# Four of the eight gated-convolution column tiles computed as block pairs in the pair stage, and a chunk loop whose exponentials are issued ahead of its fill

## The chip, the cores and the metric

The kernel runs on one core of one Trainium2 chip. The metric is the device time of one execution in microseconds, as the median of several runs. On the core, TensorE (PE) multiplies matrices, VectorE (DVE) and ScalarE (ACT) work elementwise, GpSimd (POOL) does the rest of the elementwise work, and SyncE (SP) issues the DMAs.

## The reference, cut to what matters

One layer of a hybrid decoder: a token mixer with two branches that read the same normalised input `h` (1024 positions, 1024 channels), then a gated MLP.

```python
proj = h @ w_in
z, xbc, dt_raw, sc_b, sc_c, sc_h, gates = jnp.split(proj, points, axis=-1)
y_ssd = ssd_branch(z, xbc, dt_raw, ...) @ w_ssd_out
y_sc = short_conv_branch(sc_b, sc_c, sc_h, sc_conv_w) @ w_sc_out
g_ssd, g_sc = jnp.split(jax.nn.sigmoid(gates), 2, axis=-1)
mix = (g_ssd * y_ssd + g_sc * y_sc) @ w_o

def short_conv_branch(b_gate, c_gate, h, conv_w):
    return b_gate * causal_dwconv(c_gate * h, conv_w)      # three taps
```

`ssd_branch` is a chunked scan: 4 groups of 8 heads, 8 chunks of 128 positions each. Inside a chunk the scores are weighed with exponentials of differences of a running sum, and a state is carried from chunk to chunk. The change is about the three column groups `sc_b`, `sc_c` and `sc_h` (each 1024 wide, so 8 tiles of 128 columns), and about the chunk loop.

## The kernel before, in words

Every float32 product is made of three matmuls on operands split into a high and a low part (`split`, lines 129 to 131: ACT casts the high part, DVE subtracts).

**The pair stage** (lines 583 to 628) computes two column tiles of `w_in` together. `Pair` (line 178) splits the product into 2 by 2 blocks and needs seven block products where eight would be the direct way. A block product (`product`, line 166) is 12 matmuls of 128x128 by 512, so a pair is 84 matmuls, where two tiles computed directly (`gemm`, line 158, 48 matmuls each) are 96. For this the pair needs sums of weight blocks (line 193, DVE) and seven weight splits of 512 columns (lines 130 and 131), and it takes its results from PSUM with ACT copies (line 218) and DVE additions (lines 235, 252, 256). The stage runs its pairs in the order of a string of letters (line 621): z (gate of the scan), g (merge gates) and x (scan inputs, with a four-tap convolution of 3 DVE instructions per tile).

**The chunk loop** (lines 805 to 818) runs over 32 chunks. Chunk n+1's front (`ssd_front`, line 677) loads its decay tile `E` (line 690, one of two buffers), transposes and scales the inputs. Then some steps of the fill run, then chunk n's back (`ssd_back`, line 730: 32 or 16 matmuls of line 737 into `y`, the state of lines 747 to 755, the norm of the chunk before, the output of lines 765 to 767, its square and two additions, lines 769 to 771), and then chunk n+1's decay (`ssd_decay`, line 710: exponentials on ACT at lines 716 to 726, two multiplications on DVE at lines 717 and 727, one on POOL at line 723).

**The fill** is the gated convolution: `sc_tile` (line 776) computes three column tiles directly with 48 matmuls each, and gives control back after each half (24 matmuls). `STEPS` (line 805) says how many halves run in each of eight chunks: 10 in 8 chunks, 40 in the loop. The last 8 halves run after the loop (line 822). Each column tile costs a weight split on ACT and DVE, and the three of one index share two multiplications, a copy and three taps (lines 780 to 794).

After the loop the branches (line 876) read `y_d` and `ysc_d` back from DRAM, split them (lines 842 to 853), and multiply with the output weights.

The program is written as a sequence, and a planner orders each engine's instructions by what is ready; so the order of a trace differs from that of the text. All DMAs go through SP's queue in order.

Of the kernel before, what the change touches and what calls it, by code (L numbers as in the profile page):

```python
# [8 lines left out]
F32 = mybir.dt.float32  # L9
# [3 lines left out]
ALU = mybir.AluOpType  # L13

P = 128
# [7 lines left out]
EPS = 1e-6  # L23

# [9 lines left out]
def hybrid_kernel(ctx: ExitStack, tc: tile.TileContext, x, pack, row_p, ada_w, w_in,  # L34
# [582 lines left out]

    zs = [(z_pair, g, j) for g in range(NG) for j in (0, 2)]
    xs = [(xbc_pair, g, j) for g in range(NG) for j in (0, 2, 4)]
    gs = [(gate_pair, 0, 2 * n) for n in range(8)]  # L620
    for kind in "zzggggggggxxzxzxxzxxzxxzxxzx":
        fn, g, j = dict(z=zs, x=xs, g=gs)[kind].pop(0)
        fn(g, j)
        if steps is not None:
            if next(steps, steps) is steps:
                steps = None
            last[1] = steps is not None
# [25 lines left out]
    pend = []  # L653

    late = []
# [54 lines left out]
    def ssd_decay(front):  # L710
# [3 lines left out]
        if c > 0:  # L714
            Cs = sw.tile([P, 8, P], F32, tag="Cs", name=f"Cs{nm}", bufs=2)
            S.activation(Cs, E, AF.Exp)  # L716
            V.tensor_tensor(Cs, Cs, xb[:, 5, cs].unsqueeze(1).to_broadcast([P, 8, P]), op=ALU.mult)
# [3 lines left out]
        if c < NCH - 1:  # L721
            xw = sw.tile([P, 8, 64], F32, tag="xw", name=f"xw{nm}")
# [3 lines left out]
        S.activation(E, E, AF.Exp, scale=-1.0)  # L726
        V.tensor_tensor(E, E, sm.unsqueeze(1).to_broadcast([P, 8, P]), op=ALU.mult)  # L727
        return Cs, cd, xw

    def ssd_back(front, decay):  # L730
# [37 lines left out]
        sq = scratch.rearrange("p (a b) -> p a b", a=4)  # L768
        S.activation(sq, y2, AF.Square, scale=512 ** -0.5)
        V.tensor_tensor(sq[:, 0:2, :], sq[:, 0:2, :], sq[:, 2:4, :], op=ALU.add)  # L770
        V.tensor_tensor(sq[:, 0, :], sq[:, 0, :], sq[:, 1, :], op=ALU.add)
        pend.append((sq, y2, nm, yo, g, c))
# [3 lines left out]
    def sc_tile(i):  # L776
        W = load_split(w_in[41 + i * 3], f"wsc{i}")
        pc = yield from gemm(A1p, W, f"scc{i}")
        ct = evt(f"sct{i}")
        S.copy(ct, pc)  # L780
        yield
        W = load_split(w_in[41 + i * 3 + 1], f"wsh{i}")
        ph = yield from gemm(A1p, W, f"sch{i}")
        V.tensor_tensor(ct, ph, ct, op=ALU.mult)
        w = cv["sc_w"][:, i * 3:i * 3 + 3]
        u = evt(f"scu{i}")
        S.activation(u, ct, AF.Copy, scale=w[:, 2:3])
        for k in (1, 0):
            s = 2 - k
            V.scalar_tensor_tensor(u[:, s:], ct[:, :T - s], w[:, k:k + 1], u[:, s:], op0=ALU.mult, op1=ALU.add)  # L790
        yield
        W = load_split(w_in[41 + i * 3 + 2], f"wsb{i}")
        pb = yield from gemm(A1p, W, f"scb{i}")
# [523 lines left out]
```

## Time and profile before

| | us |
|---|---|
| median of 3 runs | 2043.41 (2042.09 to 2044.56) |
| the profiled execution | 2045.67 |
| its span, first to last instruction | 2044.0 |
| PE / DVE / ACT / POOL busy | 1993.1 / 1453.3 / 978.8 / 152.0 |

The busy times are read against the span. A stage's share says more than that of the whole, so the rows further down cut the span into the stretches that the change touches. In this trace a matmul's duration includes the time in which the next one already runs, so the price of a matmul is read from one start to the next.

### The profile page before, as it was taken

The numbers are of one execution on the slowest core, as the hardware profiler recorded it, in microseconds if no ns is written. First come the engines' busy times: TensorE is split into PE (matmuls) and PEld (weight loads), VectorE is DVE, ScalarE is ACT, GpSimd is POOL, SyncE is SP. The second block draws the span as 40 slices with busy tenths as digits, with TensorE's granted clock in tenths as the row PEclk, the third lists the DMA queues.
The fourth block names the chain that finished last, engine by engine and source line by source line (L and its number), as shares of the span: only waits on it lengthen the run. The fifth ranks groups of instructions, "written<-read, shape, count | busy, mean of one in ns | idle before, by whom it ended". The sixth has DMA issues, their size and how long they took to land. (4 is left out here: it accounts for less than half of the span.)

```text
span 2044.0 us, 25283 instructions
## 1 busy us (share of the span) xinstructions
PE 1993.1 (98%) x9476; PEld 1599.2 (78%) x9476; DVE 1453.3 (71%) x2016; ACT 978.8 (48%) x1572; POOL 152.0 (7%) x183
## 2 busy tenths in 40 slices
PE   7999999999999999999999999999999999989997
PEld 3788888888887777777887878876888888868886
DVE  4966567767768787786766555378887777767876
ACT  4665455544547656554422442246554454544443
POOL 1200000000002222121000010021000000000002
PEclk9999999999999999999999999999999999999999
DMA  8233223233245556553686567252222222268362
GB/s 298 77 125 120 104 98 120 100 111 120 99 139 208 167 186 206 170 165 127 203 275 230 196 228 266 93 187 71 103 72 93 83 73 93 83 228 282 119 232 98
DMA packets 128426, 308.97 MB, mean 151 GB/s; under 512 B 11184, under 2 KB 40240, under 8 KB 128304
## 3 DMA queue, kind: packets, MB, share of 16 engines
q1 hardware_dynamic: 128304, 307.36, 43.9%
q8 instruction: 74, 1.21, 0.2%
q14 instruction: 48, 0.39, 0.1%
HBM read 241.65 MB, written 65.67 MB: 150 GB/s over the span
## 5 line engine op out<-in xcount | busy, mean ns | idle before, releaser
L1042 DVE SCALAR_TENSOR_TENSOR uv<-u_u,pk,uv 128x1023 f32<-128x1023 f32 (+1 forms) x88 | 107.2, 1279 | 7.4 <-ACT uv L1039 7.4
L130 ACT CAST u_t_hi<-u_t 128x512 fp32r<-128x512 f32 x88 | 54.7, 623 | 119.8 <-PE u_p L172 108.6
L130 ACT CAST wy_hi<-wy_raw 128x1024 fp32r<-128x1024 f32 x32 | 33.6, 1051 | 133.4 <-PE bps L858 83.4
L594 DVE SCALAR_TENSOR_TENSOR xv<-x_u,pk,xv 128x1023 f32<-128x1023 f32 (+2 forms) x72 | 87.1, 1279 | 4.9 <-ACT xv L591 4.9
L725 ACT ACTIVATE E<-E,tokS 128x128 f32<-128x128 f32 x256 | 80.5, 390 | 14.5 <-DMA E<-acs_d 13.8
L130 ACT CAST u_hi<-u_raw 128x512 fp32r<-128x512 f32 x66 | 41.0, 622 | 73.2 <-PE u_p L172 73.2
L131 DVE TENSOR_TENSOR u_t_lo<-u_t,u_t_hi 128x512 fp32r<-128x512 f32 x88 | 60.2, 687 | 21.2 <-ACT u_t_hi L130 21.1
L716 ACT ACTIVATE Cs<-E 128x1024 f32<-128x1024 f32 x28 | 29.7, 1060 | 75.3 <-DMA E<-acs_d 75.2
L131 DVE TENSOR_TENSOR wy_lo<-wy_raw,wy_hi 128x1024 fp32r<-128x1024 f32 x32 | 39.1, 1221 | 37.4 <-ACT wy_hi L130 37.4
L130 ACT CAST x_t_hi<-x_t 128x512 fp32r<-128x512 f32 x48 | 29.9, 624 | 59.2 <-PE x_p L172 33.8
L1039 ACT ACTIVATE uv<-u_u,pk 128x1024 f32<-128x1024 f32 x44 | 52.5, 1238 | 2.3 <-DVE u_u L260 1.7
L737 PE MATMUL y<-E,xdt 128*64 128x128 f32 x512 | 51.1, 279 | 1.6 <-issue 1.6
L1189 POOL TENSOR_TENSOR dss<-dss,dss 128x1 f32<-128x1 f32 x8 | 3.8, 478 | 623.4 <-PE dx L1117 600.0
L130 ACT CAST x_hi<-x_raw 128x512 fp32r<-128x512 f32 x36 | 22.4, 623 | 53.2 <-PE x_p L172 25.2
L131 DVE TENSOR_TENSOR x_t_lo<-x_t,x_t_hi 128x512 fp32r<-128x512 f32 x48 | 32.5, 687 | 21.1 <-ACT x_t_hi L130 21.1
L727 DVE TENSOR_TENSOR E<-E,sm 128x1024 f32<-128x1024 f32 x32 | 41.1, 1286 | 8.5 <-ACT E L726 8.3
L131 DVE TENSOR_TENSOR u_lo<-u_raw,u_hi 128x512 fp32r<-128x512 f32 x66 | 45.0, 684 | 2.6 <-ACT u_hi L130 2.5
L256 DVE TENSOR_TENSOR u_u<-u_p,u_q 128x512 f32<-128x512 f32 x22 | 15.2, 691 | 44.3 <-PE u_p L173 44.3
L723 POOL TENSOR_TENSOR xw<-xdt,tokS 128x512 f32<-128x512 f32 x28 | 32.4, 1157 | 187.6 <-PE st L747 158.8
L765 DVE SCALAR_TENSOR_TENSOR yo<-xb,pk,y 128x128 f32<-128x128 f32 x128 | 39.3, 341 | 7.1 <-PE y L737 6.8
L737 PE MATMUL y<-Cs,state 128*64 128x128 f32 x448 | 43.9, 273 | 0.0
L896 DVE SCALAR_TENSOR_TENSOR gt<-gt,bps 128x512 f32<-128x512 f32 x32 | 20.5, 683 | 32.5 <-PE bps L859 30.2
(1865 smaller groups left out, 6716.2 us busy)
## 6 DMA issues: line engine op xcount, KB each, us to landing
u_raw<-in_w_up_dram SPq DMA_DIRECT2D x44, 512.0 KB, 3.5
E<-acs_d SPq DMA_DIRECT2D x32, 512.0 KB, 4.7
wy_raw<-in_w_ssd_dram SPq DMA_DIRECT2D x32, 512.0 KB, 4.9
x_raw<-in_w_in_dram SPq DMA_DIRECT2D x24, 512.0 KB, 3.4
xbc_d<-xv SPq DMA_DIRECT2D x24, 512.0 KB, 2.8
xb<-xbc_d SPq DMA_DIRECT2D x16, 768.0 KB, 6.3
f_d<-uv SPq DMA_DIRECT2D x22, 512.0 KB, 2.6
dm<-f_d SPq DMA_DIRECT2D x44, 256.0 KB, 6.0
```

What stands on the lines that cost most here:

```text
L130: S.copy(hi, src)
L131: V.tensor_sub(lo, src, hi.bitcast(F32))
L594: V.scalar_tensor_tensor(v[:, s:], u[:, :T - s], w[:, k:k + 1], v[:, s:], op0=ALU.mult, op1=ALU.add)
L716: S.activation(Cs, E, AF.Exp)
L723: G.tensor_tensor(xw, xdt, bc(tS[:, 3, hs], 64), op=ALU.mult)
L725: S.activation(E[:, h, :], E[:, h, :], AF.Relu, scale=-1.0, bias=tS[:, 0, g * 8 + h:g * 8 + h + 1])
L727: V.tensor_tensor(E, E, sm.unsqueeze(1).to_broadcast([P, 8, P]), op=ALU.mult)
L737: return PE.matmul(pt[o * 64:o * 64 + 64, j * P:j * P + P], lhs[:, 2 * j + o, :], rhs[:, 2 * j + o, :], start=first, stop=last)
L765: V.scalar_tensor_tensor(yo[:, i, cs], xb[:, i, cs], cv["ssd_d"][:, g * 4 + i:g * 4 + i + 1], pt[:, i * P:(i + 1) * P], op0=ALU.mult, op1= ...
L896: V.scalar_tensor_tensor(gts[o], gts[o], 1.0, ps[:, o, :], op0=ALU.add, op1=ALU.mult)
L1039: S.activation(v, us[j], AF.Identity, scale=w[:, 2:3], bias=cv["ffn_b"][:, t:t + 1])
L1042: V.scalar_tensor_tensor(v[:, s:], us[j][:, :T - s], w[:, k:k + 1], v[:, s:], op0=ALU.mult, op1=ALU.add)
```

## The change

- Indices 0 to 3 of the gated convolution (`SCP = 4`) leave the fill. Their 12 column tiles become 6 pairs in the pair stage, two at a time between the g pairs: first the `c` and `h` columns of one index as a pair, whose product and three taps are stored to `ysc_d` (`sc_pair` with b = 0), and, for two indices, the `b` columns as a pair, which loads the stored rows again, multiplies and stores (b = 1).
- The fill keeps indices 4 to 7: 24 halves, 5 in 8 chunks (20 in the loop, 4 after it). It loads and splits the next column tile's weights half a tile ahead.
- In the loop, chunk n+1's decay is cut in two: ACT's exponentials and POOL's product come right after its front and ahead of the fill; the two DVE multiplications (`ssd_weigh`) come after the fill and ahead of chunk n's back. The square and its two additions of chunk n (`ssd_square`) move behind chunk n+2's front and decay.
- `xw` moves from a single buffer to a slot of the pool of ten.

The diff, whole:

```diff
@@ -21,6 +21,7 @@
 DFF = 2816
 KF = DFF // P
 EPS = 1e-6
+SCP = 4
 
 PACK = [
     ("c", 8), ("ada_b", 48), ("mix_pre_g", 8), ("ffn_pre_g", 8),
@@ -615,11 +616,33 @@
             S.activation(us[o], us[o], AF.Tanh, scale=0.5)
             SY.dma_start(gate_d[j + o], us[o])
 
+    def sc_taps(i, ct, u):
+        w = cv["sc_w"][:, i * 3:i * 3 + 3]
+        S.activation(u, ct, AF.Copy, scale=w[:, 2:3])
+        for k in (1, 0):
+            s = 2 - k
+            V.scalar_tensor_tensor(u[:, s:], ct[:, :T - s], w[:, k:k + 1], u[:, s:], op0=ALU.mult, op1=ALU.add)
+
+    def sc_pair(b, i):
+        if not b:
+            ct, u = Pair(A1, w_in[41 + i * 3], w_in[42 + i * 3], f"sch{i}").finish()
+            V.tensor_tensor(ct, ct, u, op=ALU.mult)
+            sc_taps(i, ct, u)
+            SY.dma_start(ysc_d[i], u)
+            return
+        us = Pair(A1, w_in[43 + i * 3], w_in[46 + i * 3], f"scb{i}").finish()
+        for o in range(2):
+            u = evt(f"scu{i + o}")
+            SY.dma_start(u, ysc_d[i + o])
+            V.tensor_tensor(us[o], us[o], u, op=ALU.mult)
+            SY.dma_start(ysc_d[i + o], us[o])
+
+    scs = [(sc_pair, b, i) for i0 in range(0, SCP, 2) for b, i in ((0, i0), (0, i0 + 1), (1, i0))]
     zs = [(z_pair, g, j) for g in range(NG) for j in (0, 2)]
     xs = [(xbc_pair, g, j) for g in range(NG) for j in (0, 2, 4)]
     gs = [(gate_pair, 0, 2 * n) for n in range(8)]
-    for kind in "zzggggggggxxzxzxxzxxzxxzxxzx":
-        fn, g, j = dict(z=zs, x=xs, g=gs)[kind].pop(0)
+    for kind in "zzgsgsgsgsgsgsggxxzxzxxzxxzxxzxxzx":
+        fn, g, j = dict(z=zs, x=xs, g=gs, s=scs)[kind].pop(0)
         fn(g, j)
         if steps is not None:
             if next(steps, steps) is steps:
@@ -650,9 +673,7 @@
         return ap.unsqueeze(2).to_broadcast([P, ap.shape[1], n])
 
     half = bank("half")
-    pend = []
-
-    late = []
+    fresh, pend, late = [], [], []
 
     def ssd_norm():
         sq, y2, nm, yo, g, c = pend.pop(0)
@@ -714,18 +735,31 @@
         if c > 0:
             Cs = sw.tile([P, 8, P], F32, tag="Cs", name=f"Cs{nm}", bufs=2)
             S.activation(Cs, E, AF.Exp)
-            V.tensor_tensor(Cs, Cs, xb[:, 5, cs].unsqueeze(1).to_broadcast([P, 8, P]), op=ALU.mult)
         if c < NCH - 1 and c > 0:
             cd = small.tile([P, 8], F32, tag="cd", name=f"cd{nm}")
             S.activation(cd, E[:, :, P - 1], AF.Exp)
         if c < NCH - 1:
-            xw = sw.tile([P, 8, 64], F32, tag="xw", name=f"xw{nm}")
+            xw = qt(f"xw{nm}").rearrange("p (h d) -> p h d", h=8)
             G.tensor_tensor(xw, xdt, bc(tS[:, 3, hs], 64), op=ALU.mult)
         for h in range(8):
             S.activation(E[:, h, :], E[:, h, :], AF.Relu, scale=-1.0, bias=tS[:, 0, g * 8 + h:g * 8 + h + 1])
         S.activation(E, E, AF.Exp, scale=-1.0)
+        return Cs, cd, xw
+
+    def ssd_weigh(front, decay):
+        nm, g, c, xb, zt, cs, hs, E, xdt, sm, Bt = front
+        Cs = decay[0]
+        if c > 0:
+            V.tensor_tensor(Cs, Cs, xb[:, 5, cs].unsqueeze(1).to_broadcast([P, 8, P]), op=ALU.mult)
         V.tensor_tensor(E, E, sm.unsqueeze(1).to_broadcast([P, 8, P]), op=ALU.mult)
-        return Cs, cd, xw
+
+    def ssd_square():
+        y2, nm, yo, g, c = fresh.pop(0)
+        sq = scratch.rearrange("p (a b) -> p a b", a=4)
+        S.activation(sq, y2, AF.Square, scale=512 ** -0.5)
+        V.tensor_tensor(sq[:, 0:2, :], sq[:, 0:2, :], sq[:, 2:4, :], op=ALU.add)
+        V.tensor_tensor(sq[:, 0, :], sq[:, 0, :], sq[:, 1, :], op=ALU.add)
+        pend.append((sq, y2, nm, yo, g, c))
 
     def ssd_back(front, decay):
         nm, g, c, xb, zt, cs, hs, E, xdt, sm, Bt = front
@@ -765,57 +799,61 @@
             V.scalar_tensor_tensor(yo[:, i, cs], xb[:, i, cs], cv["ssd_d"][:, g * 4 + i:g * 4 + i + 1],
                                    pt[:, i * P:(i + 1) * P], op0=ALU.mult, op1=ALU.add)
         V.tensor_tensor(y2, y2, zt[:, :, cs], op=ALU.mult)
-        sq = scratch.rearrange("p (a b) -> p a b", a=4)
-        S.activation(sq, y2, AF.Square, scale=512 ** -0.5)
-        V.tensor_tensor(sq[:, 0:2, :], sq[:, 0:2, :], sq[:, 2:4, :], op=ALU.add)
-        V.tensor_tensor(sq[:, 0, :], sq[:, 0, :], sq[:, 1, :], op=ALU.add)
-        pend.append((sq, y2, nm, yo, g, c))
+        fresh.append((y2, nm, yo, g, c))
 
     tail = []
 
-    def sc_tile(i):
-        W = load_split(w_in[41 + i * 3], f"wsc{i}")
-        pc = yield from gemm(A1p, W, f"scc{i}")
-        ct = evt(f"sct{i}")
-        S.copy(ct, pc)
-        yield
-        W = load_split(w_in[41 + i * 3 + 1], f"wsh{i}")
-        ph = yield from gemm(A1p, W, f"sch{i}")
-        V.tensor_tensor(ct, ph, ct, op=ALU.mult)
-        w = cv["sc_w"][:, i * 3:i * 3 + 3]
-        u = evt(f"scu{i}")
-        S.activation(u, ct, AF.Copy, scale=w[:, 2:3])
-        for k in (1, 0):
-            s = 2 - k
-            V.scalar_tensor_tensor(u[:, s:], ct[:, :T - s], w[:, k:k + 1], u[:, s:], op0=ALU.mult, op1=ALU.add)
-        yield
-        W = load_split(w_in[41 + i * 3 + 2], f"wsb{i}")
-        pb = yield from gemm(A1p, W, f"scb{i}")
-        V.tensor_tensor(u, pb, u, op=ALU.mult)
-        if i < KT - 1:
-            SY.dma_start(ysc_d[i], u)
-        else:
-            tail.append(u)
-        yield
-
     def projections():
-        for i in range(8):
-            yield from sc_tile(i)
-
-    STEPS = (0, 1, 1, 2, 1, 2, 1, 2)
+        n_sc = [(i, p) for i in range(SCP, KT) for p in range(3)]
+
+        def weights(n):
+            return load_split(w_in[41 + n_sc[n][0] * 3 + n_sc[n][1]], f"wsc{n}") if n < len(n_sc) else None
+
+        W = weights(0)
+        ct = u = None
+        for n, (i, p) in enumerate(n_sc):
+            ps = cur["pm"].tile([P, 2, 512], F32, tag="mm", name=f"sc{i}_{p}")
+            hs = [ps[:, 0, :], ps[:, 1, :]]
+            gemm_into(hs, A1p, W, 0, 4)
+            W2 = weights(n + 1)
+            yield
+            gemm_into(hs, A1p, W, 4, 8)
+            W = W2
+            ps = ps.rearrange("p a b -> p (a b)")
+            if p == 0:
+                ct = evt(f"sct{i}")
+                S.copy(ct, ps)
+            elif p == 1:
+                V.tensor_tensor(ct, ps, ct, op=ALU.mult)
+                u = evt(f"scu{i}")
+                sc_taps(i, ct, u)
+            else:
+                V.tensor_tensor(u, ps, u, op=ALU.mult)
+                if i < KT - 1:
+                    SY.dma_start(ysc_d[i], u)
+                else:
+                    tail.append(u)
+            yield
+
+    STEPS = (0, 1, 1, 0, 1, 1, 0, 1)
     proj = projections()
     chunks = [(g, c) for g in range(NG) for c in range(NCH)]
     front = ssd_front(0, 0)
     decay = ssd_decay(front)
+    ssd_weigh(front, decay)
     for n in range(len(chunks)):
         this = front, decay
         if n + 1 < len(chunks):
             front = ssd_front(*chunks[n + 1])
+            decay = ssd_decay(front)
+        if fresh:
+            ssd_square()
         for _ in range(STEPS[n % 8]):
             next(proj, None)
+        if n + 1 < len(chunks):
+            ssd_weigh(front, decay)
         ssd_back(*this)
-        if n + 1 < len(chunks):
-            decay = ssd_decay(front)
+    ssd_square()
     ssd_late()
     ssd_norm()
     ssd_late()
```

## Rows read from the trace of the kernel before

**Rows 1.** The page: span, busy times, granted clock by slice, and a convolution tap's group.

```profile
span 2044.0 us, 25283 instructions
PE 1993.1 (98%) x9476; PEld 1599.2 (78%) x9476; DVE 1453.3 (71%) x2016; ACT 978.8 (48%) x1572; POOL 152.0 (7%) x183
PEclk9999999999999999999999999999999999999999
...
L594 DVE SCALAR_TENSOR_TENSOR xv<-x_u,pk,xv 128x1023 f32<-128x1023 f32 (+2 forms) x72 | 87.1, 1279 | 4.9 <-ACT xv L591 4.9
```

**Rows 2.** Busy time in stretches: us, PE, PEld, DVE, ACT, POOL, clock, DMA, GB/s.

```profile
110.00:264.80 154.80, 154.80 (x682) 126.33 (x682) 94.28 (x144) 77.40 (x122) 0.00 (x0) 1.00 0.32 113
302.00:340.00 38.00, 38.00 (x168) 31.03 (x167) 25.23 (x34) 18.62 (x28) 0.00 (x0) 1.00 0.30 111
```

**Rows 3.** The same view: start, chunk loop, tail, and two parts of the loop.

```profile
608.50:626.10 17.60, 16.96 (x82) 13.70 (x82) 11.43 (x13) 12.18 (x22) 1.32 (x2) 1.00 0.96 328
626.10:964.40 338.30, 331.99 (x2203) 261.39 (x2202) 263.76 (x491) 192.93 (x420) 80.99 (x81) 1.00 0.52 170
964.40:1011.90 47.50, 47.04 (x235) 38.88 (x235) 34.18 (x51) 20.99 (x31) 1.10 (x2) 1.00 0.53 173
626.10:667.00 40.90, 38.73 (x286) 29.86 (x285) 35.52 (x68) 29.42 (x65) 13.33 (x14) 1.00 0.45 156
648.00:668.00 20.00, 19.92 (x154) 15.67 (x155) 18.76 (x35) 12.96 (x29) 6.12 (x6) 1.00 0.43 145
```

**Rows 4.** PE's groups in 626.1 to 964.4 without the fill's, first and last.

```profile
L737 PE MATMUL y<-E,xdt 128*64 128x128 f32 x496 | 49.5, 279 | 1.6 <-issue 1.6
...
L701 PE MATMUL half<-ident,xb 128*128 128x128 f32 x26 | 7.1, 272 | 0.0
```

**Rows 5.** Instructions of line 153, a column tile's first matmul: ns min/median/max, first and last start.

```profile
L153 PE MATMUL scc<-h_0h,wsc_hi x1: 389/389/389, 979.3 to 979.3; 128*128 128x512 f32 x1
L153 PE MATMUL scb<-h_0h,wsb_hi x1: 389/389/389, 1001.0 to 1001.0; 128*128 128x512 f32 x1
```

**Rows 6.** DVE's groups in 626.1 to 964.4: busy us, mean ns, idle before and its end.

```profile
L727 DVE TENSOR_TENSOR E<-E,sm 128x1024 f32<-128x1024 f32 x31 | 39.9, 1288 | 8.5 <-ACT E L726 8.3
...
L131 DVE TENSOR_TENSOR wsb_lo<-wsb_raw,wsb_hi 128x1024 fp32r<-128x1024 f32 x7 | 8.6, 1223 | 8.0 <-ACT wsb_hi L130 8.0
...
L131 DVE TENSOR_TENSOR wsh_lo<-wsh_raw,wsh_hi 128x1024 fp32r<-128x1024 f32 x6 | 7.3, 1219 | 0.8 <-ACT wsh_hi L130 0.8
```

**Rows 7.** Timeline: one decay tile's way from its load to its chunk.

```profile
641.39 8.71 SPq L690 DMA_DIRECT2D E<-acs_d  x2
653.69 1.06 ACT L716 ACTIVATE Cs<-E 128x1024 f32<-128x1024 f32 x1 [0.70 <-DMA E<-acs_d]
657.37 1.06 ACT L726 ACTIVATE E<-E 128x1024 f32<-128x1024 f32 x1
665.18 1.23 DVE L727 TENSOR_TENSOR E<-E,sm 128x1024 f32<-128x1024 f32 x1
667.04 0.44 PE L737 MATMUL y<-E,xdt 128*64 128x128 f32 x4
```

**Rows 8.** Timeline around the loop's end: last chunk's output, what follows, first reload split.

```profile
964.43 0.44 PE L737 MATMUL y<-E,xdt 128*64 128x128 f32 x4
...
966.33 0.49 PE L670 MATMUL half<-rs,ones 128*128 128x128 f32 x2
980.87 0.72 ACT L851 ACTIVATE y_0h<-y_r,pk 128x512 fp32r<-128x512 f32 x1 [0.78 <-DVE scu L794]
```

**Rows 9.** Two DVE lines (ns min/median/max) and POOL's two products in 626.1 to 964.4.

```profile
L727 DVE TENSOR_TENSOR E<-E,sm x31: 1209/1220/1837, 630.8 to 954.6; 128x1024 f32<-128x1024 f32 x31
L671 DVE TENSOR_TENSOR yo<-yo,half x29: 671/677/690, 643.3 to 953.8; 128x512 f32<-128x512 f32 x29
L723 POOL TENSOR_TENSOR xw<-xdt,tokS 128x512 f32<-128x512 f32 x27 | 31.3, 1161 | 178.8 <-PE st L747 158.8 <-DVE ym L662 10.2 <-DVE yo L765 5.0
L751 POOL TENSOR_TENSOR state<-state,cd 128x512 f32<-128x512 f32 x24 | 27.2, 1135 | 2.7 <-ACT cd L720 1.3 <-ACT E L726 0.9 <-DVE state L752 0.4
```

## The prediction

> **What bounds the kernel now.** I read the page first, for the share of each engine and the clock: PE is busy in 98% of the span and the granted clock stays in its top tenth in every slice [rows 1]. An edit that takes matmuls away can therefore pay, if the stretch it takes them from goes on being PE's. So the next view is the busy time cut into the stretches that the change touches. In the pair stage PE has no gap: the eight g pairs take 154.8 us with PE busy for all of it, and 38.0 us hold 168 matmuls, which are two pairs of 84 [rows 2]. DVE is busy there for 94.3 of 154.8 us and ACT for 77.4. The chunk loop, from the first matmul of the first chunk's output (626.1) to that of the last (964.4), takes 338.3 us with PE busy for 332.0 and DVE for 263.8, 78% [rows 3]. What the reader is to see is the pair of numbers 332.0 and 263.8: the loop is PE's, but DVE stands only 68 us behind, and the change takes far more from PE than from DVE.
>
> **The pair stage gains six pairs.** A pair's price is 154.8 / 8 = 19.35 us by the g pairs, and 38.0 / 2 = 19.0 us by the later ones [rows 2]; I take 19.2, so 6 x 19.2 = 115.2 us (114.0 to 116.1). This is PE's price and holds if DVE and ACT keep up. A g pair costs DVE 94.3 / 8 = 11.8 us at most, since the steps of `dt` are in that number. A c/h pair adds one product of 1024 columns (1.22, as line 727's median in [rows 9]) and two taps at 1.28 [rows 1], so 3.8 us and 15.6 in all; a b pair adds two products, 14.2 in all. Both are under 19, and they alternate with g pairs. ACT has 77.4 / 8 = 9.7 us in a g pair, of which an s pair drops the two Tanh and adds at most one scaled copy. SP's queue gets 8 stores more in this stage, 4 loads, and 12 weight loads that the fill issued before; a b pair's loads wait for stores made one or two pairs earlier, and their rows are needed only when the pair ends, 19 us after they can be issued. I cost all that at nothing: PE's 19.2 us of a pair hide it; without that cover a b pair would be late by its loads alone, bounded below in the rivals.
>
> **The fill loses 24 of 48 halves, 20 in the loop and 4 behind it.** A column tile's 48 matmuls take (1001.0 - 979.3) / 2 = 10.85 us where nothing else runs [rows 5], so a half takes 5.43. PE's floor in the loop: 332.0 - 20 x 5.43 = 223.4 us. Tail: 4 x 5.43 = 21.7 us. If everything stayed PE's, the sum would be 115.2 - 24 x 5.43 = -15.1 us, which is what 72 matmuls fewer are worth.
>
> **But the loop changes hands.** DVE's floor: PE's other groups in the loop have 1308 instructions (eight rows, first and last in [rows 4]) of 2203 [rows 3], so the fill has 895, or 37.3 halves. On DVE the fill's seven groups last 54.3 us (first and last in [rows 6]: 8.6 and 7.3) of 290.2 for all of DVE's nineteen; durations overlap where DVE runs back to back, since the union is 263.8, so the fill stands for 54.3 x 263.8 / 290.2 = 49.4 us, 1.32 per half. 20 halves less leave 263.8 - 26.5 = 237.3 us. The change takes no chunk work from DVE; the same fifteen instructions per chunk stay, only moved. So DVE's floor, 237.3, stands above PE's, 223.4: the loop becomes DVE's. How near it gets to its floor no row shows directly. Upper end: the first five chunks ran with few fill matmuls, and DVE was busy for 35.5 of 40.9 us, 87% [rows 3]; that would give 272.8 us. Lower end: DVE all but always busy, 99%, gives 239.7. I take the 20 us in which DVE really was the busier neighbour of a full PE, 18.76 of 20.0, 94% [rows 3]: the loop would take 237.3 / 0.94 = 252.5 us, 8.1 per chunk. The five early chunks, which took 8.2 us each, agree.
>
> **The moved exponentials.** Before, chunk n+1's exponentials stand behind chunk n's output in the text; after, they stand ahead of the fill, with their DVE products behind it. At 10.9 us per chunk they cost nothing; at 8.1 they matter, through `E`'s two buffers. One `E` can be followed in [rows 7]: its load is the second of two issues that end at 641.39 + 8.71 = 650.1, ACT takes 653.69 to 658.43, then the product of line 727 waits on DVE until 665.18, and the chunk's matmuls start at 667.04. From load to matmuls 17 us pass, of which 658.43 to 665.18 = 6.75 is waiting for DVE. Without that wait 10.5 us are left, and with the 1.9 us of a chunk's output matmuls (964.43 to 966.33, [rows 8]) before the buffer is free, 12.4 us for two chunks, 6.2 per chunk: below 8.1. The edit attacks just that wait, as the product now stands ahead of chunk n's output on DVE. I give it no price of its own in the forecast; it is what lets DVE reach 94%. On DVE, what is queued behind a product that waits for ACT is chunk n's state and output, and behind those the next norm; PE's next chunk needs them only through the state. The square moved behind the next front keeps ACT free for the exponentials; its reader, the norm, is two chunks late anyway. `xw`'s pool slot frees POOL, which is no bound (81.0 of 338.3 us, [rows 3]). The weight splits half a tile ahead move DVE work, they add none.
>
> **Start and tail.** The start (608.5 to 626.1) I leave at 17.6 us. The tail keeps 47.5 - 21.7 = 25.8 us. The first reload split after the loop stands at 980.87, 16.4 us after the last chunk's start at 964.43 [rows 8], so a branch that starts 25.8 us after it finds its first operands ready. I cost it at zero, with up to 5 us if DVE (busy 34.2 of 47.5 us, [rows 3]) comes late.
>
> **The sum.** Pair stage +115.2; loop 252.5 - 338.3 = -85.8; tail -21.7: +7.7 us. On the span 2044.0 + 7.7 = 2051.7; the profiled execution has 1.7 us around its span (2045.67) and lies 2.3 above the median of the runs, so against the median 2043.4 + 7.7 = **2051 us**.
>
> **A rule of the Trainium skill** bears on DVE's floor, and gives a rival below. The rows first: line 727, both of whose inputs lie in SBUF, has a median of 1220 ns and a maximum of 1837, while line 671, which reads one input from PSUM, never passes 690 around 677 [rows 9]. The Trainium skill's page "SBUF — State Buffer", section "Who interferes with whom", says that a DVE instruction with two SBUF inputs and a GpSimd instruction that reads SBUF exclude each other for their whole length, and that one with a single SBUF input doesn't contend. By that rule the trace agrees in kind; it speaks against a change that leaves DVE fewer gaps.
>
> **The rivals.** (1) *PE stays the bound, or DVE runs at its floor*: faster. For it: PE was busy 38.7 of 40.9 us in the early chunks [rows 3], and the exponentials now come early. Against it: DVE's floor lies above PE's. The loop takes 239.7 (99%) down to 229.7 (PE's floor with today's 6.3 us of gaps, if back-to-back running shortens DVE's union by what separates them), so the sum is -5 to -15; I take 2033. (2) *`E`'s two buffers become the bound*: slower. Place: the wait of line 727 on DVE. At 8.1 us per chunk the two-chunk chain of 12.4 us decides once the wait passes 16.3 - 12.4 = 3.9 us. If the 6.75 of [rows 7] survives in half of the pairs, their mean is (19.1 + 16.3) / 2 = 17.7 us, the loop 31 x 8.85 = 274, the sum +29: 2073. (3) *POOL blocks DVE*: POOL has 27 + 24 products in the loop [rows 9], and a collision costs 1837 - 1220 = 0.62 us. If half of the 51 meet a DVE product where now some 10 do (line 727's mean of 1288 is 0.07 above its median, 2 us in 31), 16 more cost 10 us, at 94% 10.6: 2062. The page above states the exclusion. (4) The change doesn't do what it says, if the planner draws the fill of the tail into the loop's gaps; then the tail pays back what the loop gains, and it ends near the forecast.
>
> **How the numbers follow.** Forecast (with 4), DVE between 90 and 97%, sum 0 to +19: 0.47. Rival 1: 0.30. Rival 2: 0.15. Rival 3: 0.08. Range 2030 to 2072: it takes in all but the ends of rivals 1 and 2. Some 0.2%, 4 us, is about what a measurement of this kernel can tell from no change. Faster by more: rival 1 nearly whole and a little of the forecast, 0.31. Within: the forecast with DVE above 95%, 0.20. Slower: the rest, 0.49.
>
> **What would show it.** Right: six pairs more at 19.2 us each with PE gapless; a loop with DVE over 90% busy and PE below it; 8.1 us from chunk to chunk. Wrong: a loop with PE at 97% or more and DVE below 95% (rival 1); ACT waiting for `E`'s load and PE for line 727 with DVE under 88% (rival 2); line 727's mean rising well over 1288 ns (rival 3); gaps on PE among the s pairs.

## The result and the profile after

The changed kernel takes 2091.4 us (2087.6 to 2096.6) beside 2043.1: a ratio of 1.0237 (95% interval 1.0213 to 1.0262), slower by 48 us where +8 was forecast. Its profiled execution is 2089.95, with a span of 2088.2, 44.2 more than before's. The page first (span, busy shares, granted clock by slice):

```profile
span 2088.2 us, 25325 instructions
PE 2006.3 (96%) x9404; PEld 1598.0 (77%) x9404; DVE 1499.0 (72%) x2088; ACT 998.2 (48%) x1622; POOL 158.0 (8%) x183
PEclk9999999999999999989999999999999999999999
```

PE has 72 matmuls fewer, yet is busy 13 us longer and idle 31 us longer. The stretches say where. The stage before the loop ends at 740.3 (was 626.1), the last chunk's output starts at 1020.2, the first branch at 1043.5. Busy time in stretches (us, then PE, PEld, DVE, ACT, POOL, granted clock, DMA share, GB/s): the first eight pairs behind the z pairs, the loop, the tail, 10 us inside the loop, and 19.3 us that begin 1.2 us after the branch does.

```profile
110.00:264.80 154.80, 154.80 (x683) 126.61 (x682) 104.18 (x153) 71.65 (x115) 0.00 (x0) 1.00 0.31 110
740.30:1020.20 279.90, 254.10 (x1759) 188.34 (x1758) 239.46 (x460) 174.23 (x403) 83.71 (x79) 0.96 0.53 179
1020.20:1043.50 23.30, 20.08 (x105) 15.63 (x104) 15.54 (x31) 5.23 (x7) 3.46 (x3) 0.93 0.34 113
794.20:804.40 10.20, 6.61 (x41) 5.26 (x41) 6.12 (x14) 4.28 (x11) 1.97 (x2) 0.50 0.35 116
1044.70:1064.00 19.30, 12.02 (x47) 8.55 (x47) 18.19 (x30) 12.94 (x23) 0.00 (x0) 0.91 0.90 302
```

Set beside [rows 2, 3], worked out from the starts of the first matmul of each stage:

| stage | before | after | difference | predicted |
|---|---|---|---|---|
| start to first chunk | 626.1 | 740.3 | +114.2 | +115.2 |
| chunk loop | 338.4 | 279.9 | -58.5 | -85.8 |
| tail | 47.5 | 23.4 | -24.1 | -21.7 |
| first branch | 137.0 | 148.7 | +11.7 | 0 (up to 5) |
| rest | 895.0 | 895.9 | +0.9 | 0 |

The pairs and the tail came as worked out. Missing are 27 us in the loop and 12 at the branch. DVE's busy time in the loop is near what was foreseen (239.5 beside 237.3), but that is 85.6% of the loop and not 94%. PE's is not: it is busy for 254.1 us, 91%, where the prediction had a floor of 223.4. Some 36 matmuls of the fill came forward from the tail (8 us), and the stretches at half clock that are shown below cost PE up to 9 (an estimate, half of its 18.3 busy us in them). The rest was not taken apart; the chunk's own matmuls last longer, as the first of these lines shows beside the 49.5 us of line 737 in [rows 4]. The second is PE's wait for `xb`, the tile with the inputs of two chunks, which experiment e3 takes up.

```profile
L771 PE MATMUL y<-E,xdt 128*64 128x128 f32 x498 | 65.0, 295 | 5.1 <-issue 5.0
L716 PE MATMUL xT<-ident,xb 128*128 128x128 f32 x120 | 19.8, 287 | 14.8 <-DMA xb<-xbc_d 14.8
```

So busy time alone does not say which engine bounds the loop; the experiments do.

Where DVE stands idle, by its groups in the loop (busy us, mean ns, idle before, what ended it), with one POOL group below; then the same two steps in the kernel before.

```profile
L753 DVE TENSOR_TENSOR Cs<-Cs,xb 128x1024 f32<-128x1024 f32 x27 | 38.7, 1434 | 0.5 <-ACT Cs L737 0.5
L132 DVE TENSOR_TENSOR wsc_lo<-wsc_raw,wsc_hi 128x1024 fp32r<-128x1024 f32 x9 | 14.8, 1646 | 0.0
L686 DVE TENSOR_SCALAR rs<-ident,yr 128x128 f32<-128x128 f32 x29 | 9.1, 315 | 11.6 <-POOL yr L122 11.5
L683 DVE TENSOR_SCALAR ym<-half 128x1 f32<-128x1 f32 x29 | 4.4, 153 | 24.1 <-PE half L681 24.1
L743 POOL TENSOR_TENSOR xw<-xdt,tokS 128x512 f32<-128x512 f32 x26 | 39.8, 1531 | 37.9 <-DVE xdt L718 37.8
```

```profile
L665 DVE TENSOR_SCALAR rs<-ident,yr 128x128 f32<-128x128 f32 x30 | 8.6, 286 | 13.3 <-POOL yr L121 13.2
L662 DVE TENSOR_SCALAR ym<-half 128x1 f32<-128x1 f32 x30 | 4.6, 153 | 3.8 <-PE half L660 3.5
```

Of DVE's 40.4 us of idle time in the loop, 35.7 stand before two small steps of the norm: 24.1 for PE's sum and 11.6 for POOL's root. The second wait was there before at nearly the same size (13.3), when a PE-bound loop hid it. The first grew from 3.8. Lines 753 and 132 read two tiles from SBUF and have longer means than their like before (1218 and 1220): nine of line 753's 27 products last 1.86 us, and each of them starts 0.6 us after an `xw` on POOL. One case of the first wait, in order of time:

```profile
789.86 0.86 DVE L799 SCALAR_TENSOR_TENSOR yo<-xb,pk,y 128x128 f32<-128x128 f32 x3
790.74 0.53 SPq L703 DMA_DIRECT2D xb<-xbc_d  x1
797.79 1.09 PE L716 MATMUL xT<-ident,xb 128*128 128x128 f32 x4 [5.13 <-DMA xb<-xbc_d]
800.05 0.16 DVE L683 TENSOR_SCALAR ym<-half 128x1 f32<-128x1 f32 x1 [3.68 <-PE half L681]
```

DVE's last reading of an old `xb` ends at 790.7, only then is the next `xb` loaded into its buffer, PE stands 5.1 us at the transposes that need it, with the norm's sum queued behind them, and DVE stands 3.7 us for that sum. PE's granted clock is at half (1.2 of 2.4 GHz) from 794.2, inside that wait, to 804.4, as the stretch above shows; there are three such stretches in the loop, 23.8 us together.

### The profile page after: what moved, and what is told of

The parts are those of the page before. It is cut to its first block, busy times and chain, and to the rows that moved or that the text cites. A ratio compares the mean times of both kernels' runs of the same rounds, so it can differ in the third digit from the quotient of the medians.

```text
span 2088.2 us, 25325 instructions
## 1 busy us (share of the span) xinstructions
PE 2006.3 (96%) x9404; PEld 1598.0 (77%) x9404; DVE 1499.0 (72%) x2088; ACT 998.2 (48%) x1622; POOL 158.0 (8%) x183
## 5 line engine op out<-in xcount | busy, mean ns | idle before, releaser
L771 PE MATMUL y<-E,xdt 128*64 128x128 f32 x512 | 66.6, 294 | 5.1 <-issue 5.0
L132 DVE TENSOR_TENSOR wy_lo<-wy_raw,wy_hi 128x1024 fp32r<-128x1024 f32 x32 | 39.0, 1220 | 40.0 <-ACT wy_hi L131 40.0
L771 PE MATMUL y<-Cs,state 128*64 128x128 f32 x448 | 61.5, 291 | 0.0
L737 ACT ACTIVATE Cs<-E 128x1024 f32<-128x1024 f32 x28 | 29.6, 1056 | 61.2 <-DMA E<-acs_d 61.2
L771 PEld LDWEIGHTS y<-E,xdt 128*64 128x64 f32 x512 | 44.4, 143 | 17.7 <-issue 14.9
L771 PEld LDWEIGHTS y<-Cs,state 128*64 128x64 f32 x448 | 45.2, 145 | 2.3 <-issue 1.7
L743 POOL TENSOR_TENSOR xw<-xdt,tokS 128x512 f32<-128x512 f32 x28 | 41.8, 1496 | 46.7 <-DVE xdt L718 46.7
```

Of the source, the lines that this page charges most:

```text
L132: V.tensor_sub(lo, src, hi.bitcast(F32))
L743: G.tensor_tensor(xw, xdt, bc(tS[:, 3, hs], 64), op=ALU.mult)
L771: return PE.matmul(pt[o * 64:o * 64 + 64, j * P:j * P + P], lhs[:, 2 * j + o, :], rhs[:, 2 * j + o, :], start=first, stop=last)
```

## The experiments

All loops, from the start of the first chunk's output to that of the last chunk's; busy times in us; ratios against the kernel before on the same chip, with the 95% interval. A loop's time is that of one profiled execution, and the executions of one kernel lie 2 to 9 us apart, so a few us between two loops say little unless the ratios differ too.

| kernel | loop | PE | DVE | DVE share | ratio |
|---|---|---|---|---|---|
| before | 338.4 | 332.0 | 263.8 | 78% | 1 |
| after | 279.9 | 254.1 | 239.5 | 86% | 1.0237 (1.0213 to 1.0262) |
| e1 order alone | 350.0 | 335.2 | 273.4 | 78% | 1.0070 (1.0051 to 1.0090) |
| e2 pairs alone | 275.3 | 243.2 | 233.8 | 85% | 1.0224 (1.0208 to 1.0239) |
| e3 third `xb` | 274.1 | 256.4 | 239.5 | 87% | 1.0182 (1.0162 to 1.0202) |
| e4 three pairs | 293.3 | 274.9 | 253.0 | 86% | 1.0070 (1.0053 to 1.0087) |
| e5 DVE loaded | 297.8 | 263.4 | 259.5 | 87% | 1.0344 (1.0323 to 1.0365) |
| e6 `Cs` on POOL | 287.3 | 245.2 | 245.6 | 85% | 1.0268 (1.0246 to 1.0289) |
| e7 three pairs, old order | 295.1 | 274.1 | 247.6 | 84% | 1.0065 (1.0049 to 1.0081) |
| e8 e7 with `Cs` on POOL | 304.4 | 273.8 | 260.4 | 86% | 1.0138 (1.0118 to 1.0157) |
| e9 no `xw` | 278.7 | 253.6 | 229.2 | 82% | 1.0213 (1.0198 to 1.0228) |
| e10 no `Cs` product | 249.7 | 233.1 | 214.1 | 86% | 1.0096 (1.0079 to 1.0113) |
| e11 third `E` | 281.4 | 259.0 | 240.0 | 85% | 1.0240 (1.0225 to 1.0255) |
| e12 longer tail | 272.2 | 236.8 | 233.9 | 86% | 1.0255 (1.0240 to 1.0271) |
| e13 fill in eighths | 279.4 | 248.3 | 240.7 | 86% | 1.0200 (1.0185 to 1.0216) |
| e14 three pairs, eighths | 292.7 | 275.5 | 253.4 | 87% | 1.0059 (1.0044 to 1.0074) |
| e15 e14 with a third `xb` | 285.3 | 273.6 | 253.7 | 89% | 1.0019 (1.0009 to 1.0030) |
| e16 e14 in the old order | 292.1 | 272.8 | 245.2 | 84% | 1.0054 (1.0035 to 1.0072) |
| e17 third `xb`, norm's steps moved | 263.1 | 248.4 | 236.9 | 90% | 1.0156 (1.0140 to 1.0171) |
| e18 e15 with the steps moved | 277.9 | 272.0 | 250.3 | 90% | 0.9995 (0.9983 to 1.0006) |

The first four took the change apart. In them theory A is PE's standing in order for `xb`, theory B that DVE bounds the loop, theory C that the new order costs.

**e1**: the new order without pairs (the string of pairs is the old one; `xw`'s slot and the early weight splits stay as changed).

```diff
-SCP = 4
+SCP = 0
...
-    STEPS = (0, 1, 1, 0, 1, 1, 0, 1)
+    STEPS = (0, 1, 1, 2, 1, 2, 1, 2)
```

> The loop's new order alone: no column tile moves to the pair stage (SCP = 0, the old string of pairs), STEPS as before (10 halves in 8 chunks). Computes the whole reference. Theory A (two buffers of xb: the load for a pair of chunks waits for line 799 of the pair before last, and PE's queue stands behind the transposes) and theory B (DVE's share alone) both leave this run PE-bound, since a chunk takes 10.9 us: 2043, within 6 us of before. Theory C (the new order itself is what harms, with or without pairs): 2055 or more.

Measured 2060.4, as theory C had it: without pairs the new loop costs 0.7%, 11.6 us of it in the loop. What costs them was not taken apart.

**e2**: six pairs, with `ssd_weigh`, `ssd_square`, `sc_tile` and `xw` as before.

> The six pairs alone: the loop's old order and the old column-tile routine, indices 4 to 7 in the fill, STEPS of the change (5 halves in 8 chunks). Computes the whole reference. Theory A and B: the order is not the cause, the loop stays near 280 us and the whole at 2085 to 2110. Theory C: the old order would have kept the gain, 2028 to 2050.

Measured 2090.6, as slow as the whole change, with DVE at 85%. With the six pairs the order makes no difference that can be measured, so theory C falls for this change.

**e3**: a third buffer for `xb`; `xdt` moves to the ten-slot pool to make room.

```diff
-            xb = ld.tile([P, 6, 256], F32, tag="xb", name=f"xb{nm}")
+            xb = ld.tile([P, 6, 256], F32, tag="xb", name=f"xb{nm}", bufs=3)
...
-        xdt = sw.tile([P, 8, 64], F32, tag="xdt", name=f"xdt{nm}", bufs=2)
+        xdt = qt(f"xdt{nm}").rearrange("p (h d) -> p h d", h=8)
```

> The changed kernel with three buffers of xb instead of two (xdt moves to the pool of ten slots to make room). Computes the whole reference. Theory A: PE's 14.8 us of waiting for xb's load go, and with them the stretches at half clock inside the loop; the loop falls from 279.9 us to 252 to 264, the whole to 2063 to 2076. Theory B: the loop stays within 4 us, the whole at 2087 to 2095.

Measured 2081.3, between the two theories. PE's 14.8 us of waiting for `xb` are gone, but its idle time in the loop falls only from 25.8 to 17.7, and its mean granted clock stays at 0.96, where theory A had the stretches at half clock go too. The loop of the profiled execution, the slowest of four, gains 5.8 us; the ratio falls by 0.0055, which is 11 us. So theory A holds for a fifth to two fifths of the missing 27 us.

```profile
L686 DVE TENSOR_SCALAR rs<-ident,yr 128x128 f32<-128x128 f32 x29 | 9.2, 316 | 12.7 <-POOL yr L122 12.6
L683 DVE TENSOR_SCALAR ym<-half 128x1 f32<-128x1 f32 x29 | 4.5, 157 | 15.5 <-PE half L681 15.4
```

These are DVE's two waits in e3: the wait for PE's sum fell from 24.1 to 15.5, that for POOL's root not at all.

The clock itself does not order the loops: e2's is shorter than the changed kernel's with a mean of 0.93 beside 0.96, and e4, next, has 1.00 and the same share of DVE, 86%.

**e4** and **e7**: three pairs, with 28 halves of the fill in the loop and 8 behind it, in the new and in the old order.

```diff
-SCP = 4
+SCP = 2
...
-    STEPS = (0, 1, 1, 0, 1, 1, 0, 1)
+    STEPS = (0, 1, 1, 1, 1, 1, 1, 1)
```

> The change at half its size: two indices (three pairs) move, 36 halves stay in the fill, 28 in the loop (7 in 8 chunks) and 8 after it as before. Computes the whole reference. PE's floor in the loop is 332 - 10 x 5.43 = 278, DVE's 264 - 10 x 1.32 = 251. Theory A and B: DVE at 90% of the loop is still possible, so PE stays the bound and the sum is 57.6 - 54 to - 60, 2036 to 2050, with the branches' start unhurt. Theory C: slower than 2055.

> Three pairs (two indices) with the loop's old order: 28 halves in the loop, 8 after it. Computes the whole reference. Theory B with 86% of DVE's 251 us: loop 292, the whole at 2053 to 2061 as in the run with the new order. Theory C' (the new order costs 12 us wherever PE still has fill enough, as it did with all the fill): the old order gives 2040 to 2050.

Measured 2058.3 and 2058.4. Alone, e4 looks like theory C, which had it slower than 2055, while theories A and B had hoped for less than 2050; e7, just as slow in the old order, rules the order out, and has the time that theory B gave it. With the tail of before, the first branch takes 135.2 and 136.6 us, where it took 137.0 before the change. The loop stands above PE's need here too, in either order.

**e5**: DVE gets a product of 512 columns more per chunk, which nobody reads.

```diff
+        idle = qt(f"idle{nm}").rearrange("p (a b) -> p a b", a=4)
+        wide = ones.unsqueeze(1).to_broadcast([P, 4, P])
+        V.tensor_tensor(idle, wide, wide, op=ALU.mult)
```

> The changed kernel with one more DVE instruction per chunk that nobody reads or waits for (a product of 512 columns, 0.6 us back to back, 19 us in the 31 chunks of the loop). Computes the whole reference. Theory B (the loop is DVE's, at about 86%): the loop grows from 279.9 by 19 / 0.86 = 22 us, the whole to 2108 to 2116. Theory A (waits on loads and on PE's queue; DVE's 40 us of idle time are slack): the loop grows by under 8 us, the whole stays at 2088 to 2099.

```profile
741.10:1038.90 297.80, 263.39 (x1764) 193.03 (x1763) 259.50 (x489) 176.45 (x403) 97.68 (x79) 0.95 0.47 161
```

DVE's busy time rises by 20.0 and the loop by 17.9: work given to DVE is paid almost whole, and the ratio, 0.0107 higher, says 22 us. **e10** takes work from it instead: the 27 products of line 753 (38.7 us) are left out.

> The changed kernel without DVE's product of line 753 (the weighing of the state's share in the output by C is left out): 27 products of 1.43 us, 38.7 of DVE's 239.4 us in the loop. Theory B (DVE is the bound at some 86%): DVE's own need falls to 200.7 / 0.855 = 235 us, below PE's 254.1 less what half clock costs it (up to 9), so PE becomes the bound: loop 246 to 256, span 2054 to 2064. Rival (chains set the loop: E's load for which ACT waits 61.2 us, xb's load for which PE waits 14.8 us): DVE's time becomes idle time, loop 270 to 280, span 2078 to 2088.

The loop falls by 30.2 to 249.7, with PE busy for 93% of it, as theory B has it. Its rival (chains set the loop) had 270 to 280 and falls. The loop falls by more than DVE's busy time (25.3); the product is also a step between ACT and PE, so e10 alone would not show that the work counts. e5's product is no such step.

**e6**: the same product on POOL instead (`G.tensor_tensor` in line 753).

> The changed kernel with the product of Cs (27 in the loop, 1.14 us each on DVE) moved from DVE to POOL. Computes the whole reference. Theory B: DVE loses 31 us, and if it keeps its 86% the loop falls from 279.9 by up to 36 us, to 244 to 262, less what POOL's reads cost DVE's products with two inputs in SBUF; the whole at 2055 to 2075. Theory A: the loop stays within 6 us or grows, since the product on POOL is slower (about 2.2 us) and stands ahead of the chunk's matmuls: 2086 to 2100.

No relief: the loop is 7.4 us longer, as theory A had it and theory B had not. On POOL a product takes 2575 ns, and DVE's others stretch meanwhile, so that DVE's busy time does not fall (245.6 beside 239.5). DVE's wait for POOL's root grows as well, from 11.6 to 21.7. What each of these costs, and whether PE's matmuls get the product late, was not taken apart. Three groups, and then one case in order of time, in which DVE's `rs` ends just behind POOL's product:

```profile
L753 POOL TENSOR_TENSOR Cs<-Cs,xb 128x1024 f32<-128x1024 f32 x27 | 69.5, 2575 | 18.0 <-ACT Cs L737 17.9
L801 DVE TENSOR_TENSOR yo<-yo,zt 128x512 f32<-128x512 f32 x30 | 27.1, 903 | 0.0
L686 DVE TENSOR_SCALAR rs<-ident,yr 128x128 f32<-128x128 f32 x29 | 25.6, 883 | 21.7 <-POOL yr L122 21.5
```

```profile
764.85 2.36 POOL L753 TENSOR_TENSOR Cs<-Cs,xb 128x1024 f32<-128x1024 f32 x1
764.92 2.38 DVE L686 TENSOR_SCALAR rs<-ident,yr 128x128 f32<-128x128 f32 x1 [0.45 <-POOL yr L122]
```

Lines 801 and 686 have 696 and 315 ns in the changed kernel. With three pairs in the old order the same move (e8) gave 1.0138, beside e7's 1.0065, where 2036 to 2050 us had been hoped for and 2055 or more named as the sign of a late product: it took 2074.0.

**e9**: POOL's `xw` left out (the state's matmul reads `xdt` unweighed), to see what its stretching of DVE costs.

```diff
-            xw = qt(f"xw{nm}").rearrange("p (h d) -> p h d", h=8)
-            G.tensor_tensor(xw, xdt, bc(tS[:, 3, hs], 64), op=ALU.mult)
+            xw = xdt
```

> The changed kernel without POOL's product xw: the state's matmul reads xdt itself, so the weighing of each position's share in the chunk's state is left out. POOL loses 26 products, 39.8 us. In the changed kernel DVE's line 753 (two SBUF inputs) has a mean of 1434 ns where it had 1218 before, and the split's line 132 has 1646 where it had 1220. Theory B with POOL's exclusion (DVE is the loop's bound and POOL's products stretch it): DVE's busy time falls by 27 x 0.216 = 5.8 us and some of 9 x 0.43 = 3.8 us, line 753 comes back to 1220 to 1280 ns, and the loop goes from 279.9 to 269 to 274 us, the span from 2088 to 2078 to 2083. Rival (POOL runs only where DVE would have waited anyway): line 753 shorter, but the loop within 278 to 281 and the span within 2086 to 2090.

```profile
L752 DVE TENSOR_TENSOR Cs<-Cs,xb 128x1024 f32<-128x1024 f32 x27 | 32.9, 1217 | 0.8 <-ACT Cs L737 0.8
L132 DVE TENSOR_TENSOR wsc_lo<-wsc_raw,wsc_hi 128x1024 fp32r<-128x1024 f32 x9 | 10.9, 1216 | 0.0
L683 DVE TENSOR_SCALAR ym<-half 128x1 f32<-128x1 f32 x29 | 4.5, 156 | 30.9 <-PE half L681 30.9
```

The products are back at 1217 (line 752 here is 753 of the changed kernel) and 1216 ns, DVE's busy time falls by 10.3, and the loop by 1.2, as the rival had it and not theory B: most of what the stretch gave back appears as waiting for PE's sum, 30.9 instead of 24.1. The stretch is real and lay where DVE would have waited. That a DVE instruction with two inputs in SBUF and a POOL instruction that reads SBUF exclude each other is what the Trainium skill's page "SBUF — State Buffer", section "Who interferes with whom", says. The runs agree, with 1434 ns beside `xw` and 1217 without it, and add that here it cost no time that can be measured.

**e11**: a third buffer for `E` (and `xdt` in the ten-slot pool, as in e3).

> The changed kernel with a third buffer for E (and xdt in the ten-slot pool, as in the run with three xb buffers, to make room). In the changed kernel ACT waits 61.2 us of the loop for E's load. The prediction's rival 2 (E's two buffers set the loop): those waits mostly go and the loop falls to DVE's 239.4 / 0.94 = 255 us or 252 to 262, span 2060 to 2070. Theory B (DVE sets it, ACT only waits because it has time to): ACT's waits shorten, the loop stays within 274 to 282, span 2082 to 2090.

281.4: of the 61.2 us that ACT waited at line 737 for `E`'s load 19.1 are left, but it now waits 56.5 us there for PE's reading of an older chunk, and the loop stays. Rival 2 of the prediction is out. The move of `xdt` is the same as in e3, so it is not what e3 gained.

**e12**: 16 halves of the fill in the loop, 8 behind it.

```diff
-    STEPS = (0, 1, 1, 0, 1, 1, 0, 1)
+    STEPS = (0, 1, 0, 1, 0, 1, 0, 1)
```

> The changed kernel with STEPS 0,1,0,1,0,1,0,1: 16 halves of the fill stand in the loop and 8 behind it, as many as before the change. If the 11.7 us that the first branch lost come from the short tail: tail 47.5 as before, first branch back to 135 to 138 (from 148.7), loop 279.9 less 2 to 3 halves of DVE's 1.32 / 0.855 = 1.5 us, 275 to 278; sum 740.3 + 276.5 + 47.5 + 136.5 + 895.9 = 2097, span 2093 to 2100. Rival (the branch comes late for the moved square and norm, whatever the tail holds): first branch 145 to 150, span 2103 to 2112.

First branch 136.7, tail 48.3: the branch's 11.7 us belong to the short tail. In the changed kernel the last norm's product (line 692) starts at 1038.7, 18.5 us after the last chunk's output begins, and PE reaches the branch at 1043.5 with DVE busy for 18.19 of the 19.3 us from 1044.7, most of it on splits, and PE for 12.02. Before the change PE had no gap in the branch's first 19.3 us:

```profile
1011.90:1031.20 19.30, 19.30 (x87) 15.95 (x86) 16.55 (x22) 5.17 (x6) 0.00 (x0) 1.00 0.91 291
```

In the changed kernel PE then waits, until 1064.94, for the split of a weight whose load is issued only at 1060.00:

```profile
1060.00 0.33 SPq L127 DMA_DIRECT2D ws_raw<-in_w_sc_dram  x1
1063.84 1.04 ACT L131 CAST ws_hi<-ws_raw 128x1024 fp32r<-128x1024 f32 x1 [4.03 <-DMA ws_raw<-in_w_sc_dram]
1064.94 0.79 PE L895 MATMUL bps<-ys_0h,ws_hi 128*128 128x512 f32 x1 [6.58 <-ACT ws_hi L131]
```

The total is no better (2098.0): what the branch gets back, the longer tail takes.

**e13**: is the missing share the fill's coarse grain? Steps of an eighth of a tile, as many in all (20 eighths and 5 halves in eight chunks both come to 120 matmuls).

```diff
-            gemm_into(hs, A1p, W, 0, 4)
-            W2 = weights(n + 1)
-            yield
-            gemm_into(hs, A1p, W, 4, 8)
+            for k in range(8):
+                gemm_into(hs, A1p, W, k, k + 1)
+                if k == 3:
+                    W2 = weights(n + 1)
+                if k < 7:
+                    yield
...
-    STEPS = (0, 1, 1, 0, 1, 1, 0, 1)
+    STEPS = (2, 3, 2, 3, 2, 3, 2, 3)
```

> The changed kernel with the same fill in finer grains: a step is one eighth of a column tile (6 matmuls) instead of a half (24), and STEPS is 2,3,2,3,... eighths per chunk instead of 0,1,1,0,1,1,0,1 halves: 20 halves in eight chunks... both give 5 halves in 8 chunks. Cut by chunks, the changed kernel's loop has 21 chunks with a half of the fill (9.71 us, PE busy 9.16, DVE 8.20) and 10 with almost none (7.61 us, PE 6.17, DVE 6.73). Theory F (the bound changes hands from chunk to chunk, PE with a half and DVE without, so the loop is a sum of each chunk's larger need): with 2 or 3 eighths in each chunk the needs lie side by side, 245 to 254 us for PE and 239 for DVE in 31 chunks, and the loop falls from 279.9 to 255 to 266, the span to 2063 to 2075. Rival (inside a chunk DVE and PE wait for each other whatever the fill, DVE never above 87%): loop 274 to 283, span 2082 to 2092.

279.4, as the rival had it. Theory F's premise was wrong. Counted from one chunk's first output to the next's, 28 of the changed kernel's 31 chunks hold 8 to 25 matmuls of the fill, and 27 of e13's hold 8 to 24: the planner had already spread it, so the text's grain decides little, and what a different spread would give is not shown. With three pairs the eighths gave 1.0059 in the new order and 1.0054 in the old (e14, e16), beside 1.0070 and 1.0065 with halves: no difference outside the intervals, and both at the rival's times (2057.9 and 2058.5). **e15** adds the third `xb` buffer to e14:

> The run with three pairs and the fill in eighths, with a third xb buffer as well (xdt in the ten-slot pool). With a half per chunk and three pairs PE waited 11.6 us in the loop for xb's load. Theory F: with the fill spread PE's front comes no earlier than the chunk before was left by DVE, so the waits for xb are already small and the third buffer gives 0 to 4 us: median 2040 to 2051. Rival (theory A, the load of xb is what couples the engines): it gives 6 to 12 us where the eighths alone gave none, median 2046 to 2053 beside 2055 to 2061.

2050.2, as theory A's side had it, with a loop 7.4 us shorter than e14's 292.7: the coupling through `xb` is worth more than theory F allowed.

**e17** and **e18**: the norm's two small DVE steps moved, on top of e3 and of e15.

```diff
         V.tensor_tensor(y2, y2, zt[:, :, cs], op=ALU.mult)
+        if summed:
+            ssd_root()
...
+        if rooted:
+            ssd_diag()
         if fresh:
             ssd_square()
```

`ssd_root` holds line 683 and POOL's root, `ssd_diag` line 686, both cut out of `ssd_norm`.

> The changed kernel with three xb buffers (loop 274.1 us alone) and the norm's two small DVE steps moved: line 683's sum (ym) behind the chunk's four products of line 799 and its multiplication with zt, line 686's diagonal (rs) behind the next chunk's front, so that DVE no longer stands at them in the middle of line 799. With three xb buffers DVE still waited 15.4 us for ym (PE's sum) and 12.6 us for rs (POOL's root, 0.41 us each). Theory G (DVE's missing share is these two waits, which DVE sits out in order): they shrink to under 8 us together, DVE is busy for 92 to 95%, and the loop takes 252 to 264 us, the span 2062 to 2074. Rival H (PE and DVE, both over 85% busy, wait for each other wherever the steps stand): the idle time goes to other waits, loop 269 to 276, span 2079 to 2087.

> The same two moved steps in the version with three pairs, the fill in eighths and three xb buffers (loop 285.3 us, PE busy 273.5, DVE waits 8.2 for ym and 12.5 for rs; median 2050.2). Theory G: DVE's waits go, PE at 273.5 us is the bound at 97 to 99%: loop 276 to 281, median 2040 to 2046, which would be level with before or a little faster. Rival H: loop 283 to 288, median 2048 to 2054.

```profile
744.30:1007.40 263.10, 248.37 (x1760) 188.04 (x1759) 236.86 (x461) 175.77 (x398) 83.18 (x79) 0.98 0.56 185
L693 DVE TENSOR_SCALAR rs<-ident,yr 128x128 f32<-128x128 f32 x29 | 16.8, 578 | 0.4 <-POOL yr L122 0.4
L731 DVE TENSOR_TENSOR sm<-half,mask 128x128 f32<-128x128 f32 x30 | 8.7, 290 | 13.2 <-PE half L729 12.0 <-PE half L727 1.2
L687 DVE TENSOR_SCALAR ym<-half 128x1 f32<-128x1 f32 x29 | 4.5, 154 | 9.1 <-PE half L681 8.7
```

These are e17's loop and DVE's three steps that wait on others (lines 686, 724 and 683 of the changed kernel). The wait for POOL's root is gone (12.7 to 0.4), the one for PE's sum is 9.1 instead of 15.5, and 13 us have come up at `sm`, which waits for PE too. The loop falls by 11.0 to 263.1, inside theory G's bounds and outside rival H's; DVE's share of 90% is below G's 92, and the waits did not shrink to G's 8 us. So G holds in part and H for the rest. How large the part is stays open: the ratio says 5 us (1.0182 to 1.0156, with intervals that meet), since e3's profiled execution was its slowest of four. Against the changed kernel the third buffer and the moved steps together give 17 us, by the loop and by the ratio. In e18 the loop falls by 7.4 to 277.9, as G had it, with PE busy for 272.0 of it, and the whole is level with the kernel before: 2042.8, ratio 0.9995 (0.9983 to 1.0006). It is the best version found, and no gain that can be measured.

```profile
682.10:960.00 277.90, 271.95 (x1917) 209.98 (x1916) 250.34 (x478) 181.69 (x411) 87.12 (x80) 1.00 0.57 191
```

## Why the prediction was wrong

- **Pair stage**: +114.2 beside +115.2, with PE busy for all of the 154.8 us shown. Right, and the costs put at nothing (SP's queue, the b pairs' loads) were nothing.
- **Tail**: -24.1 beside -21.7. Right within the planner's freedom to draw a little more of the fill forward (60 matmuls of it are left there, not 96).
- **The loop changes hands**: right in that the loop now follows DVE's work (e5, and with it e10). That DVE's busy time, 239.5, came so near the floor of 237.3 is partly luck: without `xw` it is 229.2 (e9), so some 10 us of it are stretch by POOL; the kernel before had less of that (its line 717 lay at 1218 ns where line 753 is at 1434), and the floor holds nothing for the difference. And PE did not stay below DVE: it was busy for 254.1 us and not 223.4, so two engines, both above 85%, wait for each other in order, which a floor of one engine does not contain.
- **How near DVE gets to its floor**: this step failed. I took 94% from 20 us of the loop in which PE was busy for 19.9 [rows 3]; it is 85.6%. The upper end that stood beside it, 87% from the first five chunks, was the better row, and its 272.8 us the better number. The idle time is not spread: 35.7 of 40.4 us stand at two steps that DVE meets in order, for PE's sum and for POOL's root, and 17.1 us of it were in the kernel before (lines 665 and 662), in a view that I used for busy times only. In the order of the changed kernel each chunk holds a round trip to POOL of 0.4 us in the mean, and those 11.6 us alone bring 239.5 to 251. e3 and e17 work on the two waits by their causes, and the loop goes 279.9, 274.1, 263.1; the last 10.6 us to 252.5 were not taken apart further (DVE waits 22 us there for PE's `half` at two steps).
- **The branch's start at zero**: failed, +11.7 where 5 was the end of the range. I looked at the first split's operands and not at what DVE and SP still had before them, which a tail of eight halves hides and one of four does not (e4, e7, e12). Which of the two queues costs how much was not taken apart.
- **The moved exponentials**: I gave them no price. The new loop alone, of which they are the main part, costs 11.6 us where PE bounds it (e1); with the pairs nothing that can be measured (e2).
- **The rivals**: 1 fell: it had 239.7 us at most for the loop, which took 279.9. 2 came nearest in size (2073) with the wrong mechanism: ACT did wait 61.2 us for `E`'s load and DVE was under 88%, but ACT had waited 75.2 before, PE did not wait for line 754 (line 727 before), and a third buffer gained nothing (e11). Its sum has a slip: 17 less 6.75 is 10.2 and not 10.5, which makes it about 2071. 3 saw a real stretch (`xw` 1161 to 1531 ns, line 753 1218 to 1434) that cost 1.2 us (e9). The rest, slower at 0.49, was the likeliest sign, but the range ended at 2072 because the 87% and the branch's 5 us were taken as ends and never added to each other: 272.8 - 338.3 + 115.2 - 21.7 + 5 = +33, or 2076.

## What to carry to other kernels

When an edit hands a stage from one engine to the next, the new bound's floor is its work plus the in-order round trips that it already sits out; read these from its groups' idle column in the kernel before, where the old bound hides them. It is still only a floor: here 17.1 us of such waits stood there before the change and 35.7 after it. Work that ran at the end of a stage may be the cover of the next stage's start, so cost the queues behind it before it is moved. A stretch of durations by contention is not a cost until a run without it is shorter.

## What the runs showed of the hardware

- A DVE instruction held up by POOL shows as longer, not as idle: `rs`, 286 ns, has a mean of 883 with the 1024-column product on POOL (e6), and in the case shown it ends 0.1 us after that product, so DVE's busy time is an upper bound of its work. `rs` reads one tile and one column from SBUF, not two tiles, so it does not bear out the prediction's sentence that a single input in SBUF doesn't contend.
- POOL took 2575 ns for a product that takes DVE 1217 to 1434 (e6, e9, after).
- PE's granted clock was at half for 23.8 us in the loop of the changed kernel; before, with PE busy for 98% of the loop, its mean was 1.00 [rows 3]. In the stretch shown PE stood idle from 792.7, the clock fell at 794.2, PE worked again from 797.8, and the clock rose at 804.4. The Trainium skill's page "TensorE: Matmul & The Clock Gate", section "Part 1: The HAM clock gate", says that activity releases the throttle; the trace agrees in that stretch, with 0.50 until 804.4.
